# Rotary embedding on one core: how two small tables are loaded and spread over the partitions

## The chip, the cores and the metric

The kernel runs on one core of one Trainium2 chip. Times are microseconds (us) of the device for one execution. The profile's span, from the first to the last instruction, is about 2 us shorter than the timed run; both are named where they are used.

## The reference

`x` is 16 x 512 x 1024 float32 (32 MB), 16 heads of 64. `cos` and `sin` are 512 x 32 float32 (64 KB each).

```python
x = x.reshape(batch, seq, num_heads, head_dim)
x1, x2 = x[..., :half_dim], x[..., half_dim:]
cos = cos[None, :, None, :]
sin = sin[None, :, None, :]
rotated = np.concatenate([x1 * cos - x2 * sin,
                          x1 * sin + x2 * cos], axis=-1)
```

So 33.55 MB come in and 33.55 MB go out, with little arithmetic and two small tables that every batch and every head use again.

## The kernel before

A slab is two batches, 4 MB, laid out as 128 partitions with 32 KB each: partition p holds eight sequence rows, and partitions 0 to 63 are one batch, 64 to 127 the other. Five slab buffers are loaded ahead from SyncE's ring; the sixth load has to wait for the first store.

```python
nb = 2; slots = 5
nslabs = batch // nb            # 8 slabs
rpp = nb * seq // P             # 8 rows a partition
W = rpp * dim                   # 8192 floats a partition
SP = seq // rpp                 # 64 partitions for one batch
TW = rpp * half                 # 256 floats of each table a partition
...
load(0)                         # nc.sync.dma_start(out=slab[s], in_=dram(x, s))
```

Each partition needs the eight table rows of its sequence rows, and both halves of the partitions need the same ones. The kernel before reads each table once, in another layout (four rows a partition), through GpSimd's software DMA ring, and lets TensorE copy the rows to the right partitions by matmuls with a 0/1 selection matrix:

```python
raw = singles.tile([P, 2 * TR * half], f32, tag="raw")
for i, src in enumerate((cos, sin)):
    nc.gpsimd.dma_start(out=view(raw, i * TR * half, (1, TR * half)), in_=bass.AP(
        tensor=src.tensor, offset=src.offset,
        ap=[[TR * half, P], [1, TR * half]]))
for s in range(1, slots):
    load(s)
... # pick: 0/1 matrix made on GpSimd; tab1 = raw in bf16
acc = psum.tile([P, 2 * TW], f32, tag="acc")
for i in range(2):
    for g in range(G):
        nc.tensor.matmul(view(acc, ...), view(pick, ...), view(tab1, ...), ...)
... # three VectorE operations write tab (bf16) from acc
```

The main loop works on passes of 128 x 4096 elements, two to a slab. ScalarE casts to bf16, VectorE does two products and one sum, ScalarE casts back into the slab, and after the second pass ScalarE issues the slab's store on its own ring.

```python
for i, u in enumerate(passes):
    if i + 1 < len(passes):
        cast(passes[i + 1])                       # ScalarE, slab -> xb
    ...
    nc.vector.tensor_mul(...)                     # t2 = xb * sin part of tab
    nc.vector.tensor_mul(...)                     # xb = xb * cos part of tab
    nc.vector.tensor_add(...)                     # xb = xb + swapped t2
    nc.scalar.copy(out=view(xs, k * PW, (1, PW)), in_=xu)
    if k == rpp // rows - 1:
        nc.scalar.dma_start(out=dram(out_flat, s), in_=xs)
        if s + slots < nslabs:
            load(s + slots)
```

## Time and profile before

| | kernel before |
|---|---|
| time, median of 6 runs | 162.67 us (162.44 to 163.03) |
| span in the profile | 160.8 us |
| bytes moved | 67.24 MB, 418 GB/s over the span |
| VectorE busy, ScalarE busy | 111.3 us, 114.8 us |

The page's slice view cuts the span into 40 slices of 4.0 us. Each digit is a busy share in tenths; the DMA row is the mean over the 16 DMA engines, and GB/s is what they moved.

```profile
span 160.8 us, 182 instructions
...
DVE  0003799999999999999997599907997099950000
ACT  3006939899999999999984999069990899744000
...
DMA  6999999999999999999999999999999999999993
GB/s 220 448 408 399 473 432 399 473 432 318 416 432 456 408 432 456 416 432 456 416 432 456 416 424 440 440 416 432 456 408 432 465 408 432 456 416 432 456 416 171
DMA packets 2368, 67.24 MB, mean 418 GB/s; under 512 B 288, under 2 KB 288, under 8 KB 320
```

The DMA row is 9 from the second slice to the second last. The two compute engines have holes. The DMA engines are the bound, from end to end.

The groups view gives line, engine, operation, output from inputs, count, then busy time and the mean of one in ns, then the idle time before it and what ended that.

```profile
L117 ACT CAST xb<-slab 128x4096 bf16<-128x4096 f32 x16 | 57.5, 3602 | 27.1 <-DMA slab<-in_x_dram 27.1
L137 ACT CAST slab<-xb 128x4096 f32<-128x4096 bf16 x16 | 57.6, 3603 | 4.1 <-DVE xb L133 3.9
L130 DVE TENSOR_TENSOR t<-xb,tab 128x4096 bf16<-128x4096 bf16 x16 | 36.7, 2291 | 18.8 <-ACT xb L117 18.4
```

ScalarE needs 2 x 3.6 us for a pass, 14.2 us for a slab in the timeline's cadence; a slab's 8.4 MB need 19.4 us at 432 GB/s (16 engines at the 1213 ns that a 32 KB packet takes in the packet records; the windows from 88 us on show 432 to 433 GB/s). So the compute engines wait for the DMA (27.1 us of ScalarE's idle time ends with a slab's landing).

The DMA issue view gives queue, count, KB each and the median time from issue to landing:

```profile
raw<-in_cos_dram POOLq DMA_DIRECT2D x1, 64.0 KB, 7.1
raw<-in_sin_dram POOLq DMA_DIRECT2D x1, 64.0 KB, 9.1
```

A table is 64 KB, 0.15 us of work at 432 GB/s, and yet takes 7 to 9 us. The trace's packet records, which lie below the page's views, say in part why: on one DMA engine a 4 KB table packet (159 ns), a 32 KB slab packet (1213 ns), the 4 B write of the table's semaphore (9 ns), a slab packet, the next table's packet and so on follow one another. So the rings take turns by packet here, though these packets differ in size from 4 B to 32 KB, and each step of a table costs it a slab packet's 1.2 us. The larger part is a wait before that: the first table packet starts only at 5.96 us, 4.7 us after the issue at 1.24. Nothing of this costs time in the kernel before: the table is ready at 13.5 us, when the first slab lands (timeline: start, length, instruction, idle time before it).

```profile
13.06 0.41 DVE L106 TENSOR_SCALAR tab<-acc 128x256 bf16<-128x256 f32 x1
13.50 7.11 ACT L117 CAST xb<-slab 128x4096 bf16<-128x4096 f32 x2 [11.48 <-DMA slab<-in_x_dram]
17.14 2.29 DVE L130 TENSOR_TENSOR t<-xb,tab 128x4096 bf16<-128x4096 bf16 x1 [3.67 <-ACT xb L117]
```

### The profile page before, as it was taken

The page shows a single profiled execution, that of the slowest core. Times are in us where ns is not written, and L with a number is a line of the kernel's source. Part 1 is how long each engine was busy: PE and PEld are TensorE (multiplying, and loading weights), DVE is VectorE, ACT ScalarE, POOL GpSimd, SP SyncE. Part 2 cuts the span into 40 slices and gives each one's busy share as a digit, 9 for nine tenths or more (in the row PEclk, how much of TensorE's full clock was granted, in tenths as well). Part 3 has the DMA queues.
Part 4 walks back from the last instruction along what each step waited for, and adds up shares of the span by engine and source line. Part 5 has one row for each costly group of instructions (what it writes and reads, how often), then busy time and mean ns, then how long its engine had stood idle before and what let it go on. Part 6 is the DMA issues. An engine that isn't in the chain of part 4 may idle for free.

```text
span 160.8 us, 182 instructions
## 1 busy us (share of the span) xinstructions
PE 0.6 (0%) x4; PEld 0.4 (0%) x4; DVE 111.3 (69%) x52; ACT 114.8 (71%) x33; POOL 2.3 (1%) x9
## 2 busy tenths in 40 slices
PE   0010000000000000000000000000000000000000
PEld 0000000000000000000000000000000000000000
DVE  0003799999999999999997599907997099950000
ACT  3006939899999999999984999069990899744000
POOL 5000000000000000000000000000000000000000
DMA  6999999999999999999999999999999999999993
GB/s 220 448 408 399 473 432 399 473 432 318 416 432 456 408 432 456 416 432 456 416 432 456 416 424 440 440 416 432 456 408 432 465 408 432 456 416 432 456 416 171
DMA packets 2368, 67.24 MB, mean 418 GB/s; under 512 B 288, under 2 KB 288, under 8 KB 320
## 3 DMA queue, kind: packets, MB, share of 16 engines
q1 hardware_dynamic: 1152, 33.55, 49.4%
q10 hardware_dynamic: 1152, 33.55, 48.3%
q0 software_dynamic: 64, 0.13, 0.2%
HBM read 33.69 MB, written 33.55 MB: 418 GB/s over the span
## 4 chain that ended last, share of the span: by engine, by line
DMA 47%; ACT 25%; DVE 13%; issue 6%; ACTq 0%; SPq 0%
DMA slab<-in_x_dram 25%; DMA out_dram<-slab 22%; ACT slab L137 16%; ACT xb L117 9%; DVE xb L133 4%; DVE t L130 4%; DVE xb L130 4%; ACTq L137 0%; SPq L65 0%
## 5 line engine op out<-in xcount | busy, mean ns | idle before, releaser
L117 ACT CAST xb<-slab 128x4096 bf16<-128x4096 f32 x16 | 57.5, 3602 | 27.1 <-DMA slab<-in_x_dram 27.1
L137 ACT CAST slab<-xb 128x4096 f32<-128x4096 bf16 x16 | 57.6, 3603 | 4.1 <-DVE xb L133 3.9
L130 DVE TENSOR_TENSOR t<-xb,tab 128x4096 bf16<-128x4096 bf16 x16 | 36.7, 2291 | 18.8 <-ACT xb L117 18.4
L133 DVE TENSOR_TENSOR xb<-xb,t 128x4096 bf16<-128x4096 bf16 x16 | 36.7, 2292 | 0.5
L130 DVE TENSOR_TENSOR xb<-xb,tab 128x4096 bf16<-128x4096 bf16 x16 | 36.7, 2292 | 0.5
L92 DVE CAST tab<-raw 128x256 bf16<-128x256 f32 x1 | 0.3, 294 | 11.1 <-DMA raw<-in_sin_dram 11.1
L117 ACT ACT_TABLE_LOAD x1 | 1.3, 1283 | 0.7 <-PEq L158 0.7
L102 DVE CAST tab<-acc 128x512 bf16<-128x512 f32 x1 | 0.7, 692 | 0.7 <-PE acc L96 0.7
L75 POOL DMA_DIRECT2D raw<-in_cos_dram x1 | 0.7, 674 | 0.8 <-POOLq L158 0.8
L96 PE MATMUL acc<-tab,pick 128*128 128x128 bf16 x4 | 0.6, 302 | 11.5 <-DVE tab L92 11.5
L87 POOL TENSOR_SCALAR_AFFINE_SELECT pick<-pick 128x128 bf16<-128x128 bf16 x2 | 0.5, 290 | 0.1
L75 POOL DMA_DIRECT2D raw<-in_sin_dram x1 | 0.5, 537 | 0.0
L96 PEld LDWEIGHTS <-pick 128*128 128x128 bf16 x4 | 0.4, 128 | 11.4 <-issue 8.2
L104 DVE CAST tab<-acc 128x256 bf16<-128x256 f32 x1 | 0.4, 416 | 0.0
L106 DVE TENSOR_SCALAR tab<-acc 128x256 bf16<-128x256 f32 x1 | 0.4, 414 | 0.0
L84 POOL MEMSET pick<- 128x256 bf16 x1 | 0.3, 330 | 0.0
L158 POOL MEMSET const-float32-0.0<- 128x1 f32 x1 | 0.1, 100 | 0.2 <-issue 0.2
L158 POOL MEMSET const-bfloat16-1.0<- 128x1 bf16 x1 | 0.1, 103 | 0.0
L158 POOL MEMSET const-uint8-127<- 128x1 uint8 x1 | 0.1, 103 | 0.0
L158 POOL MEMSET const-float32-1.0<- 128x1 f32 x1 | 0.1, 100 | 0.0
## 6 DMA issues: line engine op xcount, KB each, us to landing
slab<-in_x_dram SPq DMA_DIRECT2D x8, 4096.0 KB, 27.1
out_dram<-slab ACTq DMA_DIRECT2D x8, 4096.0 KB, 28.9
raw<-in_cos_dram POOLq DMA_DIRECT2D x1, 64.0 KB, 7.1
raw<-in_sin_dram POOLq DMA_DIRECT2D x1, 64.0 KB, 9.1
```

Source lines behind the costliest of these rows:

```text
L75: nc.gpsimd.dma_start(out=view(raw, i * TR * half, (1, TR * half)), in_=bass.AP(tensor=src.tensor, offset=src.offset, ap=[[TR * half, P], ...
L84: nc.gpsimd.memset(pick, 0.0)
L87: nc.gpsimd.affine_select(out=part, in_=part, compare_op=mybir.AluOpType.not_equal, fill=1.0, base=-g, pattern=[[0, P // SP], [-G, SP]], c ...
L96: nc.tensor.matmul(view(acc, i * TW + g * TR * half, (1, TR * half)), view(pick, g * P, (1, P)), view(tab1, i * TR * half, (1, TR * half)) ...
L102: nc.vector.tensor_copy(out=view(tab, 0, (hd, 2 * rpp), (1, half)), in_=view(acc, 0, (half, 2 * rpp), (1, half)))
L104: nc.vector.tensor_copy(out=view(tab, half, (hd, rpp), (1, half)), in_=view(acc, 0, (half, rpp), (1, half)))
L106: nc.vector.tensor_scalar_mul(out=view(tab, rpp * hd + half, (hd, rpp), (1, half)), in0=view(acc, TW, (half, rpp), (1, half)), scalar1=-1.0)
L117: nc.scalar.copy(out=xb[u], in_=view(slab[s], k * PW, (1, PW)))
L130: nc.vector.tensor_mul(out=t, in0=xu, in1=view(tab, a + k * rows * hd, (hd, rows), (0, nh), (1, hd)))
L133: nc.vector.tensor_add(out=xu, in0=xu, in1=view(t2, half, (hd, rows * nh), (-half, 2), (1, half)))
L137: nc.scalar.copy(out=view(xs, k * PW, (1, PW)), in_=xu)
L158: nc = _bacc.Bacc("TRN2", target_bir_lowering=False, num_devices=1)
```

## The change

The intent is to drop TensorE, PSUM, the selection matrix and the software DMA: each table is read straight into the layout that the partitions need, twice (once for each batch of the slab), by a zero-stride leading dimension in the source pattern. Each read then moves the 1 KB of one partition. Both loads go out on ScalarE's ring.

```diff
-    psum = ctx.enter_context(tc.tile_pool(
-        name="psum", bufs=1, space=bass.MemoryType.PSUM))
...
-    TR = seq // P
-    G = rpp // TR
-    raw = singles.tile([P, 2 * TR * half], f32, tag="raw")
-    for i, src in enumerate((cos, sin)):
-        nc.gpsimd.dma_start(out=view(raw, i * TR * half, (1, TR * half)), in_=bass.AP(
+    cos_sb = singles.tile([P, TW], f32, tag="cos_sb")
+    sin_sb = singles.tile([P, TW], f32, tag="sin_sb")
+    for t, src in ((cos_sb, cos), (sin_sb, sin)):
+        nc.scalar.dma_start(out=t, in_=bass.AP(
             tensor=src.tensor, offset=src.offset,
-            ap=[[TR * half, P], [1, TR * half]]))
+            ap=[[0, nb], [TW, SP], [1, TW]]))
...
-    pick = ...; tab1 = ...; acc = ...; the matmuls      (cut)
+    nc.vector.tensor_copy(out=view(tab, 0, (hd, rpp), (half, 2), (1, half)),
+                          in_=view(cos_sb, 0, (half, rpp), (0, 2), (1, half)))
+    sin_rows = view(sin_sb, 0, (half, rpp), (1, half))
+    nc.vector.tensor_copy(out=view(tab, rpp * hd, (hd, rpp), (1, half)),
+                          in_=sin_rows)
     nc.vector.tensor_scalar_mul(
-        out=view(tab, rpp * hd + half, (hd, rpp), (1, half)),
-        in0=view(acc, TW, (half, rpp), (1, half)), scalar1=-1.0)
+        out=view(tab, rpp * hd + half, (hd, rpp), (1, half)), in0=sin_rows,
+        scalar1=-1.0)
```

More of the change, by code (lines that the diff above doesn't have):

```diff
@@ L79 @@
     for s in range(1, slots):
         load(s)
-    pick = singles.tile([P, G * P], bf16, tag="pick")
-    nc.gpsimd.memset(pick, 0.0)
-    for g in range(G):
-        part = view(pick, g * P, (SP, P // SP), (1, SP))
-        nc.gpsimd.affine_select(
-            out=part, in_=part, compare_op=mybir.AluOpType.not_equal, fill=1.0,
-            base=-g, pattern=[[0, P // SP], [-G, SP]], channel_multiplier=1)
-    tab1 = singles.tile([P, 2 * TR * half], bf16, tag="tab1")
-    nc.vector.tensor_copy(out=tab1, in_=raw)
@@ L93 @@
-    acc = psum.tile([P, 2 * TW], f32, tag="acc")
-    for i in range(2):
-        for g in range(G):
-            nc.tensor.matmul(view(acc, i * TW + g * TR * half, (1, TR * half)),
-                             view(pick, g * P, (1, P)),
-                             view(tab1, i * TR * half, (1, TR * half)),
-                             start=True, stop=True)
-    tab = singles.tile([P, 2 * rpp * hd], bf16, tag="tab")
-    nc.vector.tensor_copy(out=view(tab, 0, (hd, 2 * rpp), (1, half)),
-                          in_=view(acc, 0, (half, 2 * rpp), (1, half)))
@@ L104 @@
-    nc.vector.tensor_copy(out=view(tab, half, (hd, rpp), (1, half)),
-                          in_=view(acc, 0, (half, rpp), (1, half)))
+    tab = singles.tile([P, 2 * rpp * hd], bf16, tag="tab")
+    nc.vector.tensor_copy(out=view(tab, 0, (hd, rpp), (half, 2), (1, half)),
[3 more added lines that the diff above has]
+                          in_=sin_rows)
```

## The prediction

> **What bounds it now.** The DMA engines. The 40-slice view shows the DMA row at 9 from the second slice to the second last; 67.24 MB over the span is 418 GB/s. In the packet records a 32 KB slab packet takes 1.213 us on its engine, 432 GB/s on 16. VectorE (111.3 us busy) and ScalarE (114.8 us) have slack: in the groups view a pass of 128x4096 costs VectorE three operations of 2.29 us and ScalarE two casts of 3.60 us, so a slab costs 14.2 us of compute (timeline) against 19.5 us of load and store. TensorE, selection matrix and PSUM evictions are under 3 us and end at 13.5 us, when the first slab lands anyway (chain: slab load to 13.48, cast, first product at 17.14).
>
> **What the change does.** It removes 4 matmuls, 3 PSUM evictions, a 294 ns cast and GpSimd work, none on the chain. It adds 128 KB of reads (0.3 us at 432 GB/s). By bytes nothing should move.
>
> **What decides is how the table loads are spread.** The source pattern leads with a zero-stride dimension of 2. [...] No transfer of the kernel before has such a shape, so its trace cannot confirm it. Both tables then go to two engines, 130 ring entries on each with the semaphore writes. [...] a 4 KB table packet, a slab packet, the 4 B semaphore write, a slab packet take turns; so 64 KB took 7.1 and 9.1 us from issue to landing.
>
> **Sum (an estimate from those durations).** I take each 1 KB descriptor to be a packet. While five slab loads are queued, 45 slab-ring entries per engine (about 52 us) let some 45 table packets through. The other 85 run alone from 52.5 us at some 0.05 us each (159 ns for 4 KB and 1213 ns for 32 KB give 46 ns for 1 KB): landing near 57.5 us instead of 10.6. Three VectorE table operations take about 1 us. The first product starts at about 59 us instead of 17.1. The first store goes out 17 us later, near 76 instead of 34.4, so the DMA engines idle from about 52 to 77 us. Then stores are issued every 14.2 us at best: the eighth at 59 + 17 + 7x14.2 = 175, ending some 13 us later behind its predecessor: span 189 us, time 190 us. Of the 42 us delay some 28 remain; the slack between 14.2 and 19.5 us a slab absorbs the rest.
>
> **Predicted: 190 us, 174 to 203.** Faster 1%, within 2% 14%, slower 85%.
>
> **What would show it.** Table issues: landing 50 us or more after issue, 1 KB packets on two engines. VectorE: one idle stretch of over 40 us at the start, released by the sin table. DMA row: empty slices between about 52 and 77 us, near full later. ScalarE: three early casts, then a wait for VectorE.
>
> **What would make it wrong.** If the tables spread over 16 engines, 18 entries each land near 25 us; the first store at 42 us still precedes the end of the five loads (about 50 us), the engines never idle, and the time stays near 163 us. If several descriptors make one packet, the tables land earlier: at four a turn near 45 us, about 177 us; at sixteen or more nothing changes. If lone 1 KB descriptors cost 0.15 us, about 198 us.

59 + 17 + 7 x 14.2 us to the eighth store and some 13 us for its end come to a span of 189 us and a time of 190 us. That each table goes to two engines was then an assumption that no trace at hand showed; the 130 entries an engine and the 85 left over rest on it. That the rings take turns by packet is seen in the trace of the kernel before.

## The result, and the profile after

| | before | after |
|---|---|---|
| time, median of 6 runs | 162.67 us | 190.80 us (189.74 to 191.36) |
| span in the profile | 160.8 us | 188.7 us |
| first VectorE product starts | 17.14 us | 59.13 us |
| first store issued | 34.41 us | 76.40 us |
| eighth store issued | 146.70 us | 175.6 us |

The ratio is 1.172, 95% interval 1.169 to 1.175. A ratio is the mean time of one kernel's fast runs over that of the other's fast runs in the same rounds, so it is not quite the ratio of the medians above. The start times are from the timelines.

The slice view after, slices of 4.7 us:

```profile
span 188.7 us, 165 instructions
...
DVE  0000000000005999999999999999999999994000
ACT  2019370000000058999999999999999999975200
...
DMA  6999999999810000796999999999999999999995
GB/s 222 446 440 439 419 397 411 440 425 433 377 39 13 0 0 0 333 445 222 333 438 424 410 417 424 445 445 445 445 445 424 431 417 410 431 445 445 445 445 222
DMA packets 2564, 67.37 MB, mean 357 GB/s; under 512 B 260, under 2 KB 516, under 8 KB 516
```

There is a hole in the DMA row, from the twelfth to the sixteenth slice. Stage windows measure it. The columns are start and end, length, busy us (and instructions) of VectorE, ScalarE and GpSimd, the clock, the DMA share and GB/s:

```profile
37.00:52.00 15.00, 0.00 (x0) 0.00 (x0) 0.00 (x0) 1.00 0.99 419
52.00:58.00 6.00, 0.43 (x1) 0.00 (x0) 0.00 (x0) 1.00 0.11 41
58.00:77.00 19.00, 18.27 (x10) 7.84 (x3) 0.00 (x0) 1.00 0.00 0
77.00:90.00 13.00, 12.42 (x7) 12.95 (x4) 0.00 (x0) 1.00 0.89 363
90.00:140.00 50.00, 48.44 (x22) 49.85 (x16) 0.00 (x0) 1.00 1.00 425
```

By 52 us the five slab loads are done, but for the last packets of two engines (the last ends at 54.4 us). From 52 to 58 us the DMA engines run at 11%, which is under two engines of 16; then nothing moves until 77 us. Idle time is 6 x 0.89 + 19 + 13 x 0.11 = 25.8 us. The remainder of the 27.9 us between the spans is busy time: the packet records of all 16 engines, summed and divided by 16, are 157.5 us busy and 0.8 us idle before, 159.4 and 26.9 after (idle counted from the first packet to the last). Of the 1.9 us of added busy time 1.5 us are 32 KB packets that took longer and 0.4 us the smaller table packets.

After the hole another engine sets the pace: from 90 to 140 us ScalarE is busy 49.85 of 50 us, and the eight stores are issued 14.2 us apart, from 76.40 to 175.64 us. So from the first product on, the end is 17.3 us to the first store, seven steps of 14.2 us, and 13 us for the last store: 130 us in all.

The waits view names who waited for whom: total us, times, longest.

```profile
DVE tab L81 <- DMA cos_sb<-in_cos_dram: 55.8, 1, 55.8
ACT slab L116 <- DVE xb L112: 45.1, 3, 40.6
...
DVE tab L84 <- DMA sin_sb<-in_sin_dram: 2.3, 1, 2.3
```

VectorE waits 55.8 us for the cos table and 2.3 us more for the sin table; ScalarE waits behind VectorE. The timeline shows the moment (start, length, instruction, idle time before it):

```profile
55.83 0.43 DVE L81 CAST tab<-cos_sb 128x512 bf16<-128x512 f32 x1 [55.83 <-DMA cos_sb<-in_cos_dram]
58.52 0.29 DVE L84 CAST tab<-sin_sb 128x256 bf16<-128x256 f32 x1 [2.26 <-DMA sin_sb<-in_sin_dram]
58.73 0.29 DVE L86 TENSOR_SCALAR tab<-sin_sb 128x256 bf16<-128x256 f32 x1
59.13 2.29 DVE L109 TENSOR_TENSOR t<-xb,tab 128x4096 bf16<-128x4096 bf16 x1
...
76.28 3.60 ACT L96 CAST xb<-slab 128x4096 bf16<-128x4096 f32 x1
76.40 0.35 ACTq L118 DMA_DIRECT2D out_dram<-slab  x1
```

The product itself has not changed, 2.29 us. A caution on views: the chain of waits puts 30% of this span down to "another core or an unknown queue" (its pieces there, 0.68 to 55.8 and 56.3 to 58.5 us, are the waits for these two loads), and the issue view leaves the landing time out. The waits view has it.

The queue view shows the number of engines: 1412 packets on ScalarE's ring, where eight stores account for 8 x (128 + 16) = 1152. The other 260 are 256 reads of 1 KB and 4 semaphore writes, two for each table, where a slab, moved by all 16 engines, has 16 and each table of the kernel before had 16 too (32 of the 64 packets on its software ring). So each table uses two engines; the share of 0.11 from 52 to 58 us and the two series of starts below say the same.

```profile
q1 hardware_dynamic: 1152, 33.55, 42.9%
q10 hardware_dynamic: 1412, 33.82, 41.6%
```

The packet records show what decides. Starts of 1 KB table packets, in us from the span's start, on the two engines together:

```
 6.47  6.77  7.72  8.02  8.97  9.27 10.22 10.52 11.48 11.78 ...   (one per engine every 1.25 us)
... 50.26 50.57 51.54 51.84 52.80 53.10 | 54.05 54.10 54.15 54.19 54.23 54.27 ... 58.01
                          last slab packet ^ then one every 0.043 us on an engine
```

While slab packets are queued, an engine lets through one 1 KB packet for each 32 KB packet here, every 1.25 us. By 52.5 us only 80 of 256 have come through; once the slab ring is empty, the other 176 need 5 us.

### The profile page after: what moved, and what is told of

Same layout as the page of the kernel before. It is cut to its first block, busy times and chain, and to the rows that moved or that the text cites. A ratio compares the mean times of both kernels' runs of the same rounds, so it can differ in the third digit from the quotient of the medians.

```text
span 188.7 us, 165 instructions
## 1 busy us (share of the span) xinstructions
DVE 110.6 (59%) x51; ACT 114.6 (61%) x33; POOL 0.2 (0%) x4
## 3 DMA queue, kind: packets, MB, share of 16 engines
q1 hardware_dynamic: 1152, 33.55, 42.9%
q10 hardware_dynamic: 1412, 33.82, 41.6%
## 4 chain that ended last, share of the span: by engine, by line
ACT 39%; another core or an unknown queue 30%; issue 12%; DVE 11%; ACTq 0%; DVEq 0%
ACT slab L116 25%; ACT xb L96 14%; DVE t L109 4%; DVE xb L112 4%; DVE xb L109 4%; DVE tab L81 0%; DVE tab L84 0%; DVE tab L86 0%; ACTq L116 0%; DVEq L109 0%
## 5 line engine op out<-in xcount | busy, mean ns | idle before, releaser
L96 ACT CAST xb<-slab 128x4096 bf16<-128x4096 f32 x16 | 57.5, 3601 | 13.2 <-DMA slab<-in_x_dram 13.2
L81 DVE CAST tab<-cos_sb 128x512 bf16<-128x512 f32 x1 | 0.4, 427 | 55.8 <-DMA cos_sb<-in_cos_dram 55.8
```

Of the source, the lines that this page charges most:

```text
L81: nc.vector.tensor_copy(out=view(tab, 0, (hd, rpp), (half, 2), (1, half)), in_=view(cos_sb, 0, (half, rpp), (0, 2), (1, half)))
L96: nc.scalar.copy(out=xb[u], in_=view(slab[s], k * PW, (1, PW)))
```

## The experiments

Theory T: the zero-stride leading dimension confines each table load to two engines; there it takes turns, packet by packet, with 32 KB slab packets, and lands only when the slab ring is empty; the late table delays the first store beyond the end of the loads, and the DMA engines run dry.

Rivals: (R1) 1 KB reads or the doubled table bytes are slow as such. (R2) ScalarE's ring is the wrong place. (R3) The imbalance of two engines with extra work costs the time, not the late first product. (R4) The late first product could be caught up, and something else is lost.

### The same reads over 16 engines

```diff
     for t, src in ((cos_sb, cos), (sin_sb, sin)):
-        nc.scalar.dma_start(out=t, in_=bass.AP(
-            tensor=src.tensor, offset=src.offset,
-            ap=[[0, nb], [TW, SP], [1, TW]]))
+        for b in range(nb):
+            nc.scalar.dma_start(out=t[b * SP:(b + 1) * SP, :], in_=bass.AP(
+                tensor=src.tensor, offset=src.offset,
+                ap=[[TW, SP], [1, TW]]))
```

> The changed kernel with each table's load cut in two, one per 64 partitions, so that the source no longer leads with a dimension of 2; same ring, same 256 reads of 1 KB. Theory (two engines, one packet a turn): 16 engines share the loads, 20 table entries each at about 1.26 us a turn, tables landed at about 25 to 31 us, first product at about 26 to 32 us, DMA engines never idle, time 162.5 to 165 us. Rivals: if 1 KB reads or the doubled table bytes are what is slow, or if the place in ScalarE's ring is, the tables still land near 58 us and the time stays near 190 us.

Measured: 165.32 us against 162.98, ratio 1.014. The issue view now gives landing times:

```profile
cos_sb<-in_cos_dram ACTq DMA_DIRECT2D x2, 64.0 KB, 13.7
sin_sb<-in_sin_dram ACTq DMA_DIRECT2D x2, 64.0 KB, 24.4
```

The first product starts at 29.98 us. Same ring, same 256 reads of 1 KB, same bytes, and all but 2.3 of the 28 us are gone: R1 and R2 cannot explain them. The landing fits 16 engines: 16 reads and 4 semaphore writes an engine, at 1.25 us a turn, are 25 us (an estimate from the turns of the changed kernel). Those 2.3 us over the kernel before are a bit more than expected. The packet records show no more idle time (0.9 us) but 2.4 us more busy time, 1.9 us of it in the 32 KB packets: 101 of them took over 1300 ns, where the kernel before has 36 and the changed kernel 77. Why packets stretch was not isolated.

### Two engines, but no turns to take

```diff
-    load(0)
     ...
-        nc.scalar.dma_start(out=t, in_=...)     # pattern unchanged, leading dimension of 2
+        nc.sync.dma_start(out=t, in_=...)
+    load(0)
```

> The changed kernel with its table loads as they are, on two engines, but issued in SyncE's ring ahead of the first slab load, so that no slab packet stands between table packets. Theory: 130 entries at 46 ns, tables landed at about 8 us; the slab shares of the two engines start 6 us late and the two engines stay 6 us behind, first cast at about 18 us, time about 168.5 us (166 to 171). If two engines alone were the cost without the turns, the tables would stay late and the time near 190 us; if the two engines catch up, 163 us.

Measured: 168.04 us, ratio 1.033. Ahead of the slabs in one ring, the tables land early although they still use two engines:

```profile
6.50 0.43 DVE L80 CAST tab<-cos_sb 128x512 bf16<-128x512 f32 x1 [6.50 <-DMA cos_sb<-in_cos_dram]
10.27 0.29 DVE L83 CAST tab<-sin_sb 128x256 bf16<-128x256 f32 x1 [3.34 <-DMA sin_sb<-in_sin_dram]
```

The rest, 5.1 us, is what these loads cost at the head of the ring. The first slab lands at 19.9 us instead of 13.5; these 6.4 us are about the 6 us that 130 table entries of 46 ns take on each of the two engines. But not all of it is due to two engines: the same reads over 16 engines at the same place cost 2.4 us (165.20 us, below), which leaves about 2.8 us for the two engines. So the two factors are apart: without turns, two engines cost at most 5 us, and taking turns with slab packets raises this to 28.

### The slow loads, with nobody waiting for them

```diff
 (kernel before)
+    dead_c = singles.tile([P, TW], f32, tag="dead_c")
+    dead_s = singles.tile([P, TW], f32, tag="dead_s")
+    for t, src in ((dead_c, cos), (dead_s, sin)):
+        nc.scalar.dma_start(out=t, in_=bass.AP(
+            tensor=src.tensor, offset=src.offset,
+            ap=[[0, nb], [TW, SP], [1, TW]]))
```

> The kernel before, with the two-engine table loads added in ScalarE's ring into tiles that nothing reads. Theory (the late first product is what costs): VectorE starts at 17 to 18 us as before; the two engines carry 6 us more, and the stores queue behind the table entries in the ring, so first store landed about 8 us later: time 166 to 172 us. Rival (the two busy engines themselves cost the 28 us): near 190 us.

Measured: 168.84 us, ratio 1.036. VectorE starts at 17.23 us. R3 falls as the cause of 28 us. But the run is less clean than planned: a store's issue blocked ScalarE.

```profile
34.61 18.18 ACTq L147 DMA_DIRECT2D out_dram<-slab  x1
...
52.83 3.60 ACT L145 CAST slab<-xb 128x4096 f32<-128x4096 bf16 x1 [14.74 <-issue]
```

Issuing a store takes 0.34 to 0.38 us in the kernel before. Here it took 18.18 us, behind two loads on the same ring of which most packets had not left yet, and ScalarE's casts stood behind it until 52.8 us. (What ended the hold is not known: 176 of the 256 table packets were still to come then.) Its share of the 5.9 us is not known.

### A late first product without any slow load

```diff
 (kernel before)
     tab = singles.tile([P, 2 * rpp * hd], bf16, tag="tab")
+    nc.vector.tensor_copy(out=view(tab, 0, (1, 1)), in_=view(slab[2], 0, (1, 1)))
```

The table's first element is overwritten right after, so the result stays correct; the copy only holds VectorE until slab 2 has landed. The second run takes `slab[3]`.

> The kernel before, its tables loaded and spread as before, but VectorE builds the table only after slab 2 (the third) has landed: a one-column copy ahead of it. No table load is slow here. Theory (a late first product costs only what exceeds the slack before the five loads run out): first product at about 34 us, first store at about 51 us, just when the loads end; end 130 us after the first product: time 163 to 167 us.

Measured: 168.18 us, ratio 1.034; first product at 34.79 us, span 166.0 us.

> The same, but after slab 3 (the fourth) has landed. Theory: first product at about 44 us, DMA engines idle for some 10 us before the first store, end 130 us after the first product: time 174 to 178 us. If a late start can be caught up because 19.5 us of transfer a slab stand against 14.2 us of compute, about 165 us. If the slow table loads cost something beyond the late start, this run falls below the line that the changed kernel lies on.

Measured: 178.36 us, ratio 1.096; first product at 44.41 us, span 176.2 us. They are 1.2 and 0.4 us above the expected ranges. The hole in the DMA row is back, with every table load as fast as before:

```profile
DMA  7899998999950059599999999999999999999993
```

R4 falls: a late start is not caught up, though a slab needs 14.2 us of compute against 19.4 us of transfer. Together with the other late runs there is a line:

| run | first product S | span | span - S |
|---|---|---|---|
| before, held until slab 2 | 34.8 | 166.0 | 131.2 |
| after, 8 KB slab packets (below) | 41.0 | 171.2 | 130.2 |
| before, held until slab 3 | 44.4 | 176.2 | 131.8 |
| after, software ring (below) | 48.7 | 178.9 | 130.2 |
| after | 59.1 | 188.7 | 129.6 |

Beyond the slack, each microsecond of delay costs about one: 24.3 us between the first and the last row cost 22.7 us. The reason is ScalarE's pace: in all five runs the stores go out 14.2 us apart or a little more, so the 130 us after the first product hardly shrink. The kernel before would sit at 17.1 + 130 = 147 us on this line, but the DMA needs 160.8. So about 14 us of delay are free (first product up to about 31 us; the 16-engine run at 29.98 us agrees), and 42 - 14 = 28 us are paid. The slack is not simply the time until the five loads run out, as the expectation for the slab 2 run had it: there the first store went out at 53.1 us, about when the loads ended, and 5.2 us of span were lost all the same.

### Smaller slab packets: a dose for the turns

If turns go by packets, as the records above show, smaller slab packets must let the tables through sooner, though two engines and all bytes stay. The first try cut each of the first five slab loads into four loads:

```diff
-        nc.sync.dma_start(out=slab[s], in_=dram(x, s))
+        pieces = 4 if s < slots else 1
+        n = W // pieces
+        for j in range(pieces):
+            nc.sync.dma_start(out=view(slab[s], j * n, (1, n)),
+                              in_=dram(x, s, j * n, n))
```

> The changed kernel with each of the first five slab loads cut into four loads of a quarter of the columns, so 8 KB packets in place of 32 KB, same bytes. Theory (one table packet for each slab packet): a turn is about 0.32 us instead of 1.26 us, 130 turns end at about 45 us, first product at about 46 to 48 us, end 130 us after it: time about 178 us (175 to 182). If the turns go by bytes or time and not by packets, the tables land at 57 us as before and the time stays near 190 us.

Measured: 177.00 us, ratio 1.084. The time is in the expected range, but for another reason: the tables landed at about 21 and 24 us, not 45. SyncE's ring waits show that its later loads stood waiting for the tables:

```profile
SPq L66 <- DMA cos_sb<-in_cos_dram: 17.4, 1, 17.4
```

The slab ring ran empty at about 17.5 us, and the tables slipped through. (Why SyncE waits for a table there is not in the trace; 22 loads were issued at the start instead of 7.) So the time proves nothing here. What counts is the rate before that: from 4 to 16 us, 81 table packets on two engines and 585 slab packets of 8 KB on 16, so 40 and 37 an engine, about one for one, a turn of 0.3 us instead of 1.25.

The repeat keeps one load a slab but walks the row in pieces from the back. The pieces went as packets of their own: SyncE's ring shows 3072 packets with four pieces and 5632 with eight, instead of 1152:

```diff
+        n = W // 4                       # 8 in the second run
+        back = [[-n, 4], [1, n]]
+        nc.sync.dma_start(                # first five slabs only
+            out=view(slab[s], W - n, *back),
+            in_=bass.AP(tensor=x.tensor,
+                        offset=x.offset + s * nb * seq * dim + W - n,
+                        ap=[[W, P], *back]))
```

> The run with quartered slab loads again, without its confusion (SyncE's later loads waited there for the tables): each of the first five slab loads stays one load, but walks its row in four quarters from the back, so that it is 32 packets of 8 KB an engine instead of 8 of 32 KB. Theory (one table entry for each slab packet): the earlier run showed 3.0 turns a us at this size, so 130 turns take some 43 us, tables landed at about 48 us, first product at about 50 us, span 130 us longer than that: 180 us, time about 182 us (179 to 185). If turns went by bytes or by time, landing at 57 us or later and 190 us.

Measured: 173.21 us, ratio 1.064. The sin table is there at 40.4 us, 18 us earlier than in the changed kernel:

```profile
40.37 0.29 DVE L93 CAST tab<-sin_sb 128x256 bf16<-128x256 f32 x1 [23.01 <-DMA sin_sb<-in_sin_dram]
```

The direction is right, but the landing was expected at 48 us. The records show where the difference arose: only 41 slab packets had started by 4 us (88 in the first try), and 42 of the 130 table entries of an engine were through by 8 us. After that it is about one for one. The span lies on the line of the table above.

> The same with eight pieces, packets of 4 KB. Theory: a turn of 159 + 46 ns, 130 turns in 26 to 27 us, tables landed at about 31 us, first product at about 32 us, early enough that the transfer engines do not run dry; the smaller packets cost the loads some 2.5 us: time 165 to 169 us, though both tables still come over two engines. If two engines as such, or bytes, decide, near 190 us.

Measured: 177.30 us, ratio 1.090, a clear miss in the time, and the most instructive run. The last table packet left at 25.3 us and the first product started at 26.65 us, early enough. The loss comes later, by the same turns with the roles exchanged: slab loads of 4 KB packets now stand against stores of 32 KB packets. From 48 to 56 us the records count 96 packets of 4 KB and 96 of 32 KB, one for one. The fifth slab, queued at the start, gets its last packet at 90.6 us. The windows show compute engines starving behind it at full DMA, and the DMA then running short near the end:

```profile
56.00:74.00 18.00, 17.50 (x9) 17.95 (x6) 0.00 (x0) 1.00 0.96 403
74.00:91.00 17.00, 8.45 (x4) 5.27 (x2) 0.00 (x0) 1.00 1.04 443
91.00:140.00 49.00, 41.25 (x18) 42.56 (x12) 0.00 (x0) 1.00 1.00 429
140.00:150.00 10.00, 4.64 (x3) 8.35 (x3) 0.00 (x0) 1.00 0.44 190
```

### The software ring with the same pattern

```diff
-        nc.scalar.dma_start(out=t, in_=bass.AP(      # leading dimension of 2 kept
+        nc.gpsimd.dma_start(out=t, in_=bass.AP(
```

> The changed kernel with its table loads, leading dimension of 2 and all, issued from GpSimd's software ring. The kernel before shows this ring putting eight 512 B rows into one 4 KB packet; with four 1 KB rows a packet, two engines and one turn a packet: 33 to 66 entries on an engine, tables landed at about 45 to 57 us, time 177 to 190 us. If the software ring spreads the load over 16 engines, 6 entries each, landed at about 10 us, time 162 to 164 us.

Measured, one single look without a state: 180.86 us. The first product starts at 48.66 us. The records show 64 packets of 4 KB (four rows each) going through two at a time from 6.4 to 47.0 us, one per engine about every 1.3 us. With 64 packets of 4 KB in place of 256 of 1 KB the first product starts 10.5 us earlier than in the changed kernel (48.66 against 59.13), and GpSimd's ring, too, moves this pattern only two packets at a time here.

### Two versions without turns and with 16 engines

Both use the two-part loads of the first experiment in SyncE's ring. The first puts them ahead of slab 0, the second between slab 0 and slab 1.

> The changed kernel with its table loads cut in two and issued in SyncE's ring ahead of the first slab load: 16 engines, no slab packet between. Theory: 20 entries at 46 ns, tables landed by 4 us, slab loads about 1 us later than before, first product at about 18 us: time 162.5 to 164.5 us, the same as the kernel before, without TensorE and software DMA.

Measured: 165.20 us, ratio 1.015, more than expected. The first product starts at 19.41 us, which is harmless, but the first 10 us have 1.7 us of idle DMA time per engine instead of 0.2: so most of the 2.4 us are lost there, with the small reads at the head.

> The changed kernel with its table loads cut in two (16 engines), in SyncE's ring, behind the first slab load and ahead of the second. Theory: no taking of turns and no late start of the first slab: tables landed at about 13 us with the first slab, first product at about 17.5 us, time 162.5 to 164 us: equal to the kernel before, and less than the 165.2 us of the same loads ahead of the first slab, if what that run lost was the start (1.5 us more idle time in its first 10 us).

Measured: 162.49 us against 162.79, ratio 0.9985, interval 0.9966 to 1.0005: the same as the kernel before, without TensorE, PSUM and software DMA.

```profile
DMA  7999999999999999999999999999999999999994
...
cos_sb<-in_cos_dram SPq DMA_DIRECT2D x2, 64.0 KB, 12.1
sin_sb<-in_sin_dram SPq DMA_DIRECT2D x2, 64.0 KB, 11.5
```

The tables land with the first slab, and the first product starts at 16.87 us. Nothing beat the kernel before; its DMA engines idle 0.8 us in all, so there is next to nothing left to gain by moving tables.

## Why the prediction was right

The time was predicted at 190 us and measured at 190.8. Point by point:

- *Two engines.* An assumption; no trace of the kernel before has such a shape. The trace after shows it: two semaphore writes a table, DMA share 0.11 while only tables move. The 16-engine run shows what it is worth: 165.32 us against 190.80.
- *One packet a turn.* The kernel before showed it with 4 KB table packets. The trace after agrees: one 1 KB packet for each 32 KB packet, every 1.25 us. Packets of 8 KB made the turns shorter (0.3 us), and 4 KB against 32 KB went 96 to 96.
- *45 let through, 85 left over.* Measured: 40 data packets per engine by 52.5 us, 24 + 64 left; the first table packet left only at 6.47 us. The lone packets took 46 ns, as estimated. At that price five packets more or less are 0.2 us, so the landing hardly depends on the count of turns; it depends on when the slab ring runs empty on these two engines, which was at about 54 us and not 52.5. The landing was at 58.0 us, predicted 57.5. The terms as written, 52.5 + 85 x 0.05, give 56.8; that 57.5 was put down covered part of the ring's delay, which is luck.
- *First product 59 us, first store 76 us, DMA idle from 52 to 77 us, eighth store 175 us.* Measured 59.13, 76.40, nearly idle from 52 and wholly from 58 to 77, 175.6. One sign differs: VectorE's long wait ended with the cos table, not the sin table, which came 2.7 us later.
- *28 of 42 us remain.* Measured 27.9 between the spans, 26.0 as idle time of the DMA engines and 1.9 as more busy time. The prediction had no term for longer packets and needed none: its sum went along the compute (59 + 17 + 7 x 14.2 + 13), which is what set the end. The held runs show the same slope with no slow load at all, and put the free delay at about 14 us.

What was left out of the prediction: the two engines' extra 6 us. Without turns they cost at most 5 us (168.04 us). In the changed kernel nothing of this shows (its span - S is the lowest of the table); they are spent before the first store, when all engines are about to idle.

## What to carry to other kernels

When a small load goes out beside a bulk stream, look in a trace at how many engines it spreads over (here two, by two semaphore writes a table), and at how many packets of the other ring it lets pass (here 40 an engine by 52.5 us, 1.25 us each): the turns counted, not the bytes. Here a leading broadcast dimension of two copies was better written as two loads whose outermost dimension is 64 (165.32 us against 190.80); put behind the first bulk load in the same ring they were there by 14.3 us, about when the first slab landed (13.2 us), and cost nothing (162.49 us against 162.79). A delay at the start of a DMA-bound pipeline is free only as long as the compute that is left after it still fits under the transfer time (here 130 us under 160.8, so about 14 us); after that nearly all of it is paid (22.7 of 24.3 us in the held and late runs).
